# Moving eight merge-gate products ahead of retention, and pooling behind it, in a two-layer hybrid decoder step

## The chip, the cores and the metric

One core of a Trainium2 chip runs the whole step. The metric is the device time of one execution in microseconds (us). TensorE (PE) multiplies, VectorE (DVE) and ScalarE (ACT) work on elements, GpSimd (POOL) does the same more slowly and issues some DMAs, and SyncE (SP) issues the DMAs that load weights.

## The reference, cut to what matters

For each of two layers, over 320 tokens (256 of a prompt, 64 of samples):

```
h = x @ w_in                          # 13824 columns, split into
qa, ka, va, ga, ub, gb, qc, kc, vc, gc, ma, mb, mc = split(h)
ya = (rmsnorm(retention(qa, ka, va)) * silu(ga)) @ w_ret_o
yb = (pool(ub) @ w_pool_map * scale * silu(gb)) @ w_pool_o
yc = (window_attention(qc, kc, vc) * silu(gc)) @ w_att_o
merged = sigmoid(ma) * ya + sigmoid(mb) * yb + sigmoid(mc) * yc
x = layer_norm(alpha * x + merged @ w_out)
```

The three branches do not depend on each other, so their input products may be computed in any order, as long as each branch's parts come in its own order.

## The kernel before, in words

All tensors lie transposed: 128 features on the partitions, 320 tokens along the free axis. Every matrix is cut into 128x128 blocks, and eight blocks form a *chunk* of weights, loaded by one 512 KB DMA that SP issues (`load`, L139). The fp32 product is made of three matmuls on high and low parts. For each chunk ACT makes the high part (`split_h`, L148, tile `h`), a copy rounded to fp32r, and DVE subtracts it from the weight to give the low part (`split_l`, L156, tile `l`). A block then costs three 128x128x320 matmuls (`block`, `block_low`), a chunk 24 of them.

The loop in `run` (from L330) works off a fixed list of output products, `layer_groups()` (L51). In the middle of it each chunk's parts are made two chunks ahead: `split_h(c + 2)` at the start of a chunk, `split_l(c + 2)` and `load(c + 6)` at its middle. A product such as `("ub", 3)` takes 16 blocks (two chunks); `y*` products take 8, `pm` products 2. When a product's last matmul is issued, its `done_` function takes it out of PSUM. What must happen before a product's first block stands in `before` (L462).

Attention and the four retention heads run beside the products in *lanes*: generators whose steps are issued by `pump` (L275) at the end of each chunk. `pump` keeps a planned backlog of ACT, DVE and POOL in `self.busy`, takes `CHUNK_US` off it for each chunk, and steps a lane only if the planned backlogs of ACT and DVE are under `LATE_US`. The pooling of one `ub` product sits in a list called misc, which is stepped at every chunk whatever the backlog. All queues work in the order of the program, so an instruction that waits holds up everything behind it on its engine.

In `split_l` (L156 to L167) the plan may send a low part to POOL: if DVE's planned backlog is over 0.5 and POOL has none.

The order before in each layer: attention's `qc`, `kc`, `vc`; eight `ub` (pooling inputs) directly after them, while the second half of attention is in its lane; then `qa`, `ka`, `va` of four heads, with the eight `pm` (pooling map) products between them; then `gb`; then `mb` and `yb` alternating in pairs; then the same for branches a and c; then `wo`.

`done_mb` (L961) puts the gate's sigmoid into a small tile `sig`; `done_yb` (L969) multiplies it with yb into `acc` (four large tiles, taken at `yb` 0, L471). `done_ub` (L669) copies the product with its history into `ext` and, for the first one, loads `hist` by DMA; `pooling` (L687) forms window sums (`win`, one addition for each doubling of the window: 1, 2, 3 or 4 by group), the result `pp` and its parts `pt`. `done_pm` (L716) scales into `preB`; `gate` (L658) makes silu(g) times the branch and its high and low parts (`gbh`, `gbl`).

Large tiles come from one pool of 24 buffers (`gran`, L100), among them `x` (8 while a layer's inputs are used), attention's and retention's tiles, `hist`, `pout`, `pt`, `preB`, `oA`, `oC`, `acc`. A new tile waits until the previous holder of its buffer is done with.

Of the kernel before, what the change touches and what calls it, by code (L numbers as in the profile page):

```python
# [11 lines left out]
F32 = mybir.dt.float32  # L12
F32R = mybir.dt.float32r
AF = mybir.ActivationFunctionType
ALU = mybir.AluOpType
# [6 lines left out]
T = NP + NB * NT  # L22
# [29 lines left out]
def layer_groups():  # L52

    g = [[("kc", 0), ("vc", 0), ("qc", 0), ("qc", 1)]]
    g += [[("qc", t)] for t in (2, 3)]
    g += [[("kc", 1)], [("vc", 1)]] + [[("qc", t)] for t in (4, 5, 6, 7)]
    late = [("ub", i) for i in range(8)]
    for h in range(HA):
        late += [("qa", h), ("ka", h), ("va", 2 * h), ("va", 2 * h + 1)]
    for i, job in enumerate(late):  # L60
        g.append([job])
        if i in (4, 6, 8, 10):
            g += [[("pm", i - 4)], [("pm", i - 3)]]
    for b in "bac":
        g += [[("g" + b, i)] for i in range(8)]
        for j in range(0, 16, 2):
            g += [[("m" + b, j)], [("m" + b, j + 1)], [("y" + b, j)], [("y" + b, j + 1)]]
    g += [[("wo", j)] for j in range(16)]
    return g


def layer_blocks():

    out = []
    for grp in layer_groups():
        for k in range(n_k(grp[0][0])):
            out += [(kind, i, k) for kind, i in grp]
    return out
# [19 lines left out]
class Step:  # L98
# [57 lines left out]
    def split_l(self, c, parts=((0, CH),)):  # L156
        if c < NCHUNK:
            if c not in self.L:
                lo = self.lp.tile([128, CH, 128], F32R, tag="l", name="l")
                self.L[c] = lo  # L160
            eng = None
            if c > 8 and self.busy["v"] > 0.5 and self.busy["p"] < 0:
                eng = self.nc.gpsimd
            for i, j in parts:
                self.tt(self.L[c][:, i:j], self.raw[c][:, i:j], self.H[c][:, i:j].bitcast(F32), ALU.subtract, eng)
                if j == CH:
                    self.raw.pop(c)  # L167

# [165 lines left out]
    def run(self):  # L334
# [30 lines left out]
        for layer in range(DEPTH):  # L365
            if layer:
                self.begin_layer(layer)
            for grp in layer_groups():
                jobs = [Job(kind, i) for kind, i in grp]
                self.before(jobs[0].kind, jobs[0].i)  # L370
                for k in range(n_k(grp[0][0])):
                    if len(jobs) > 1:
                        self.need_x(min(k + 3, 15))
                    for n, job in enumerate(jobs):
                        if pos == 0:
                            self.split_h(c + 2)
                        if pos == CH // 2:
                            self.split_l(c + 2)
                            self.load(c + 6)
                        self.block(job, k, c, pos)  # L380
                        pos += 1
                        if n == len(jobs) - 1:
                            self.block_low(jobs, k)
                        if pos == CH:
                            pos = 0
                            self.H.pop(c)
                            self.L.pop(c)
                            c += 1
                            self.pump()
# [42 lines left out]

    def begin_layer(self, l):
        self.l, zs = l, getattr(self, "z", None)
        self.gated, self.pt, self.acc, self.sig = {}, {}, None, {}
        self.xk = 0
        self.x_gen = self.x_from_input() if l == 0 else self.norm(l - 1, zs, False)
        self.oC = [None, None]
        self.att = {}
        self.ret = {}  # L440
        self.preB = None
        self.oA = None
# [19 lines left out]
    def before(self, kind, i):  # L462
        if kind[0] == "g" and i == 0:
            for lane in {"gb": (), "ga": ("ret0", "ret1"), "gc": ("att",)}[kind]:
                self.drain(lane)
            self.gated[kind[1]] = self.pair(2, kind)
        if kind == "mb" and i == 0:
            for o, src in (("o_wkc", "ckr"), ("o_wvc", "cvr")):
                self.nc.gpsimd.dma_start(out=self.io[o][self.l], in_=self.io[src][self.l, :, NT:, :])
        if kind == "yb" and i == 0:  # L470
            self.acc = [self.g([128, 4, T], name=f"acc{n}") for n in range(4)]  # L471
        if kind == "yc" and i == 0:
            self.merged = self.pair(4, "mg")
        if kind == "wo" and i == 0:
            self.z = [self.g([128, 4, T], name=f"z{n}") for n in range(4)]
# [488 lines left out]
        self.act(out=t, in_=ps, func=AF.Sigmoid)  # L964
        self.sig[j] = t

    done_mb = done_mc = done_ma

    def done_yb(self, j, ps):  # L969
        self.tt(self.acc[j // 4][:, j % 4, :], self.sig.pop(j), ps, ALU.mult)  # L970

    def done_ya(self, j, ps):
        t = self.m([128, T], name="ya")
# [311 lines left out]
```

## Time and profile before

| | |
|---|---|
| median of 3 runs | 2310.35 us (2309.80 to 2310.91) |
| the profiled execution's own time | 2310.74 us |
| its span, first to last instruction | 2309.0 us |
| busy: PE, DVE, ACT, POOL | 2273.1, 1222.3, 945.8, 182.9 us |
| mean granted TensorE clock | 0.992 |
| weight low parts: made by DVE, by POOL | 562, 35 |

The span is the stretch between the first and the last instruction; 1.7 us of the profiled execution lie around it. Layer 0 ends at about 1144 us, layer 1 repeats the same order. The chain of waits follows the end of the kernel back to what released each step.

### The profile page before, as it was taken

The page shows a single profiled execution, that of the slowest core. Times are in us where ns is not written, and L with a number is a line of the kernel's source. Part 1 is how long each engine was busy: PE and PEld are TensorE (multiplying, and loading weights), DVE is VectorE, ACT ScalarE, POOL GpSimd, SP SyncE. Part 2 cuts the span into 40 slices and gives each one's busy share as a digit, 9 for nine tenths or more (in the row PEclk, how much of TensorE's full clock was granted, in tenths as well). Part 3 has the DMA queues.
Part 4 walks back from the last instruction along what each step waited for, and adds up shares of the span by engine and source line. Part 5 has one row for each costly group of instructions (what it writes and reads, how often), then busy time and mean ns, then how long its engine had stood idle before and what let it go on. Part 6 is the DMA issues. An engine that isn't in the chain of part 4 may idle for free.

```text
span 2309.0 us, 37695 instructions
## 1 busy us (share of the span) xinstructions
PE 2273.1 (98%) x15660; PEld 2218.0 (96%) x15660; DVE 1222.3 (53%) x1826; ACT 945.8 (41%) x1536; POOL 182.9 (8%) x190
## 2 busy tenths in 40 slices
PE   8999999999999999999999999999999999999997
PEld 8997999999999999999998989999999999999997
DVE  4568465443444444446665775553434434444566
ACT  4544445333433343333365444443334333433333
POOL 1114000000000000000031230000000000000001
PEclk9999999999999999999999999999999999999998
DMA  7433455444444444444353344554444444444442
GB/s 274 137 137 131 163 189 179 155 151 146 147 154 150 152 146 153 149 151 151 129 196 119 131 136 153 194 183 150 152 148 154 146 149 143 157 154 146 146 150 98
DMA packets 97628, 354.91 MB, mean 154 GB/s; under 512 B 11521, under 2 KB 11969, under 8 KB 97393
## 3 DMA queue, kind: packets, MB, share of 16 engines
q1 hardware_dynamic: 93312, 335.87, 43.5%
q0 software_dynamic: 4144, 16.64, 2.0%
q8 instruction: 122, 2.00, 0.4%
q14 instruction: 50, 0.40, 0.1%
HBM read 338.51 MB, written 17.88 MB: 154 GB/s over the span
## 4 chain that ended last, share of the span: by engine, by line
PE 93%; DVE 5%; ACT 0%; DMA 0%; issue 0%; SPq 0%; DVEq 0%
PE d L196 87%; PE p L196 4%; DVE win L182 1%; PE p L205 1%; PE p L200 1%; DMA w<-w 0%; DVE sc L191 0%; DVE l L182 0%; DVE s L186 0%; DVE z L182 0%; DVE s L182 0%; DVE s L752 0%; DVE pp L186 0%; DVE sc L186 0%; DVE pp L182 0%
## 5 line engine op out<-in xcount | busy, mean ns | idle before, releaser
L196 PE MATMUL d<-xh,h 128*128 128x320 f32 x3424 | 1073.4, 314 | 15.6 <-ACT xh L175 6.9
L182 DVE TENSOR_TENSOR l<-w,h 128x1024 fp32r<-128x1024 f32 (+1 forms) x562 | 699.3, 1245 | 724.6 <-ACT h L175 723.7
L196 PE MATMUL d<-xh,l 128*128 128x320 f32 x3424 | 1060.5, 310 | 0.9 <-DVE l L182 0.9
L196 PE MATMUL d<-xl,h 128*128 128x320 f32 x3424 | 1050.2, 310 | 0.0
L175 ACT ACTIVATE h<-w 128x1024 fp32r<-128x1024 f32 (+1 forms) x597 | 627.5, 1052 | 495.1 <-PE d L196 363.1
L196 PEld LDWEIGHTS d<-xh,h 128*128 128x128 f32 x3424 | 645.3, 188 | 28.5 <-ACT xh L175 7.8
L196 PEld LDWEIGHTS d<-xh,l 128*128 128x128 f32 x3424 | 645.5, 189 | 2.1 <-DVE l L182 1.8
L196 PEld LDWEIGHTS d<-xl,h 128*128 128x128 f32 x3424 | 642.1, 188 | 0.0
L196 PE MATMUL d<-mgh,h 128*128 128x320 f32 x512 | 158.8, 310 | 0.0
L196 PE MATMUL d<-mgh,l 128*128 128x320 f32 x512 | 158.3, 309 | 0.0
L196 PE MATMUL d<-mgl,h 128*128 128x320 f32 x512 | 158.3, 309 | 0.0
L175 ACT ACTIVATE sig<-d 128x320 f32<-128x320 f32 x96 | 42.0, 437 | 226.0 <-PE d L196 226.0
L182 POOL TENSOR_TENSOR l<-w,h 128x1024 fp32r<-128x1024 f32 x35 | 84.9, 2432 | 226.6 <-ACT h L175 191.5
L196 PEld LDWEIGHTS d<-mgh,h 128*128 128x128 f32 x512 | 96.1, 188 | 0.2
L196 PEld LDWEIGHTS d<-mgh,l 128*128 128x128 f32 x512 | 96.1, 188 | 0.2
L196 PEld LDWEIGHTS d<-mgl,h 128*128 128x128 f32 x512 | 96.1, 188 | 0.0
L182 POOL TENSOR_TENSOR acc<-acc,ya 128x320 f32<-128x320 f32 x32 | 28.2, 880 | 822.2 <-DVE ya L182 822.2
L196 PE MATMUL d<-gch,l 128*128 128x320 f32 x256 | 79.2, 309 | 0.0
L196 PE MATMUL d<-gah,h 128*128 128x320 f32 x256 | 79.2, 309 | 0.0
L196 PE MATMUL d<-gal,h 128*128 128x320 f32 x256 | 79.2, 309 | 0.0
L196 PE MATMUL d<-gbh,h 128*128 128x320 f32 x256 | 79.2, 309 | 0.0
L196 PE MATMUL d<-gcl,h 128*128 128x320 f32 x256 | 79.2, 309 | 0.0
(234 smaller groups left out, 2119.3 us busy)
## 6 DMA issues: line engine op xcount, KB each, us to landing
w<-w SPq DMA_DIRECT2D x595, 512.0 KB, 3.3
s<-s SPq DMA_DIRECT2D x16, 512.0 KB, 5.6
o_rets<-s POOLq DMA_DIRECT2D x16, 512.0 KB, 5.1
bias<-bias_p SPq DMA_DIRECT2D x8, 512.0 KB, 5.5
o_x<-z SPq DMA_DIRECT2D x8, 320.0 KB, 2.2
ck<-ck SPq DMA_DIRECT2D x4, 512.0 KB, 4.7
cv<-cv SPq DMA_DIRECT2D x4, 512.0 KB, 6.1
xin<-x SPq DMA_DIRECT2D x3, 640.0 KB, 11.8
```

Of the source, the lines that this page charges most:

```text
L175: self.nc.scalar.activation(out=out, in_=in_, func=func, **kw)
L182: (eng or self.nc.vector).tensor_tensor(out=out, in0=a, in1=b, op=op)
L196: self.nc.tensor.matmul(out, lhsT=lhsT, rhs=rhs, start=start, stop=stop)
L200: self.nc.tensor.matmul(out, lhsT=lhsT, rhs=rhs, start=False, stop=True, skip_group_check=True)
L205: self.nc.tensor.transpose(out, in_, ident[:n, :n])
```

## The change

In each layer the first eight merge-gate products of branch b (`mb` 0 to 7) come straight after attention's inputs, where the pooling inputs were. Retention's inputs follow, then the pooling inputs in pairs, with `mb` 8 to 11 and the pooling maps between them, then the remaining `mb`; then all `gb`, then all sixteen `yb`. Branches a and c stay as they were.

The gates now go straight into `acc`, which is taken a quarter at a time at `mb` 0, 4, 8 and 12. Gates 0 to 7 are copied raw, and their sigmoid is taken in place, over two tiles of 128x1280, just before `mb` 8; gates 8 to 15 get their sigmoid on the way out of PSUM. `done_yb` multiplies in place. Two DMAs that copy cache rows from HBM to HBM move from `mb` 0 to `gb` 0. Low parts of weights are always made by DVE.

```diff
-    late = [("ub", i) for i in range(8)]
+    late = [("mb", j) for j in range(8)]
     for h in range(HA):
         late += [("qa", h), ("ka", h), ("va", 2 * h), ("va", 2 * h + 1)]
-    for i, job in enumerate(late):
-        g.append([job])
-        if i in (4, 6, 8, 10):
-            g += [[("pm", i - 4)], [("pm", i - 3)]]
-    for b in "bac":
+    for n in range(4):
+        late += [("ub", 2 * n), ("ub", 2 * n + 1), ("mb", 8 + n)]
+        if n:
+            late += [("pm", 2 * n - 2), ("pm", 2 * n - 1)]
+    late += [("mb", 12), ("mb", 13), ("pm", 6), ("pm", 7), ("mb", 14), ("mb", 15)]
+    g += [[job] for job in late]
+    g += [[("gb", i)] for i in range(8)]
+    g += [[("yb", j)] for j in range(16)]
+    for b in "ac":
...
-            eng = None
-            if c > 8 and self.busy["v"] > 0.5 and self.busy["p"] < 0:
-                eng = self.nc.gpsimd
...
-        if kind == "mb" and i == 0:
+        if kind == "gb" and i == 0:
             for o, src in (("o_wkc", "ckr"), ("o_wvc", "cvr")):
...
-        if kind == "yb" and i == 0:
-            self.acc = [self.g([128, 4, T], name=f"acc{n}") for n in range(4)]
+        if kind == "mb" and i % 4 == 0:
+            self.acc.append(self.g([128, 4, T], name=f"acc{i // 4}"))
+        if kind == "mb" and i == 8:
+            for n in range(2):
+                self.act(self.acc[n], self.acc[n], AF.Sigmoid)
...
+    def done_mb(self, j, ps):
+        self.act(self.acc[j // 4][:, j % 4, :], ps, AF.Copy if j < 8 else AF.Sigmoid)
+
     def done_yb(self, j, ps):
-        self.tt(self.acc[j // 4][:, j % 4, :], self.sig.pop(j), ps, ALU.mult)
+        a = self.acc[j // 4][:, j % 4, :]
+        self.tt(a, a, ps, ALU.mult)
```

## Rows read from the trace of the kernel before

**Rows 1.** The page's first part: busy time, share of the span, instructions.

```profile
PE 2273.1 (98%) x15660; PEld 2218.0 (96%) x15660; DVE 1222.3 (53%) x1826; ACT 945.8 (41%) x1536; POOL 182.9 (8%) x190
```

**Rows 2.** Waits of PE: total us, times, longest.

```profile
PE d L196 <- ACT xh L175: 6.9, 3, 5.0
PE d L196 <- DVE rt L182: 6.7, 2, 3.3
```

**Rows 3.** Windows: length, PE, PEld, DVE, ACT, POOL busy, clock, DMA share, GB/s.

```profile
60.00:140.00 80.00, 80.00 (x565) 72.45 (x564) 44.34 (x109) 40.52 (x107) 8.98 (x9) 1.00 0.41 137
160.00:180.00 20.00, 19.33 (x117) 17.09 (x116) 19.34 (x36) 9.54 (x34) 8.17 (x4) 1.00 0.30 106
180.00:200.00 20.00, 18.66 (x133) 16.14 (x131) 19.41 (x39) 8.28 (x20) 9.73 (x5) 1.00 0.29 99
200.00:220.00 20.00, 16.23 (x122) 15.18 (x123) 19.17 (x49) 10.00 (x30) 9.52 (x8) 1.00 0.35 120
240.00:400.00 160.00, 160.00 (x1193) 151.06 (x1192) 90.03 (x161) 76.48 (x138) 10.69 (x20) 1.00 0.53 180
1300.00:1320.00 20.00, 19.52 (x119) 17.35 (x119) 19.30 (x40) 9.92 (x33) 7.19 (x3) 1.00 0.29 95
1320.00:1340.00 20.00, 19.05 (x137) 16.76 (x135) 19.41 (x40) 8.95 (x23) 9.35 (x4) 1.00 0.27 91
1340.00:1360.00 20.00, 16.53 (x108) 15.11 (x109) 19.20 (x46) 10.11 (x30) 11.03 (x9) 0.83 0.40 133
```

**Rows 4.** The timeline of PE around its longest stop in layer 1.

```profile
1341.96 0.31 PE L196 MATMUL d<-pt,h 128*128 128x320 f32 x1
1345.61 0.64 PE L196 MATMUL d<-xh,h 128*128 128x320 f32 x1 [3.34 <-DVE rt L182]
```

**Rows 5.** Windows of PE alone, then of all engines at the norm: PEclk of stretches.

```profile
1344.60:1351.40 6.80, 5.79 (x37) 0.51 0.37 145
...
1150.00:1160.00 10.00, 8.73 (x42) 8.59 (x42) 9.19 (x16) 7.57 (x14) 10.00 (x11) 0.65 0.01 2
```

**Rows 6.** Timelines of DVE and POOL: start, us, instruction, xcount.

```profile
194.79 0.63 DVE L182 TENSOR_TENSOR win<-ext 128x454 f32<-128x454 f32 x1
195.45 6.04 DVE L182 TENSOR_TENSOR win<-win 128x452 f32<-128x452 f32 x3
...
195.08 5.27 POOL L182 TENSOR_TENSOR l<-w,h 128x1024 fp32r<-128x1024 f32 x2 [8.28 <-ACT h L175]
...
1331.56 1.94 DVE L182 TENSOR_TENSOR win<-win 128x452 f32<-128x452 f32 x3
```

**Rows 7.** Groups by line and form, with the tile view's POOL row second.

```profile
L182 DVE TENSOR_TENSOR l<-w,h 128x1024 fp32r<-128x1024 f32 x560 | 697.9, 1247 | 717.2 <-ACT h L175 716.2 <-issue 0.3
...
L182 POOL TENSOR_TENSOR l<-w,h x35: 2342/2401/2760, 90.9 to 1364.5; 128x1024 fp32r<-128x1024 f32 x35
...
L175 ACT ACTIVATE h<-w 128x1024 fp32r<-128x1024 f32 x595 | 626.3, 1054 | 490.5 <-PE d L196 363.1 <-issue 93.1 <-ACT h L175 16.8
L175 ACT ACTIVATE sig<-d 128x320 f32<-128x320 f32 x96 | 42.0, 437 | 226.0 <-PE d L196 226.0
L175 ACT ACT_TABLE_LOAD x26 | 33.4, 1283 | 11.0 <-PE d L196 9.9 <-PEq L1259 0.7
```

**Rows 8.** The chain of waits: start, us, what (products of later stages).

```profile
404.68 637.12 PE d L196 x4344
```

**Rows 9.** Groups of pooling's instructions on DVE; the second is the tile view's.

```profile
L182 DVE TENSOR_TENSOR win<-ext 128x454 f32<-128x454 f32 x16 | 10.0, 623 | 0.0
...
L182 DVE TENSOR_TENSOR win<-win x24: 617/629/2708, 142.5 to 1343.6; 128x452 f32<-128x452 f32 x12, 128x448 f32<-128x448 f32 x8, 128x440 f32<-128x440 f32 x4
...
L191 DVE TENSOR_SCALAR preB<-d,pscale 128x320 f32<-128x320 f32 x16 | 8.0, 542 | 0.0
...
L182 DVE TENSOR_TENSOR pt<-pp,pt 128x320 fp32r<-128x320 f32 x16 | 7.7, 482 | 0.0
L186 DVE SCALAR_TENSOR_TENSOR pp<-win,ext 128x256 f32<-128x256 f32 x16 | 6.8, 426 | 0.7
```

**Rows 10.** DVE's timeline where the first pooling history is loaded, layer 0.

```profile
123.24 0.22 DVE L679 COPY ext<-hist 128x120 f32<-128x120 f32 x1 [5.89 <-DMA hist<-pool]
```

**Rows 11.** Timelines of ACT and DVE at layer 0's last gb product.

```profile
411.76 0.44 ACT L175 ACTIVATE gt<-d 128x320 f32<-128x320 f32 x1 [2.41 <-PE d L196]
...
413.25 0.49 DVE L182 TENSOR_TENSOR gbl<-gt,gbh 128x320 fp32r<-128x320 f32 x1 [0.54 <-ACT gbh L175]
```

**Rows 12.** Timelines of POOL and DVE at the start of layer 1.

```profile
1174.16 5.02 POOL L182 TENSOR_TENSOR l<-w,h 128x1024 fp32r<-128x1024 f32 x2 [0.63 <-ACT h L175]
...
1171.30 8.23 DVE L182 TENSOR_TENSOR xl<-z,xh 128x320 fp32r<-128x320 f32 x4
```

**Rows 13.** Issues of retention's output DMA: xcount, KB, us to landing.

```profile
o_rets<-s POOLq DMA_DIRECT2D x16, 512.0 KB, 5.1
```

More of the change, by code (lines that the diff above doesn't have):

```diff
@@ L160, in split_l @@
                 self.L[c] = lo
-            eng = None
-            if c > 8 and self.busy["v"] > 0.5 and self.busy["p"] < 0:
-                eng = self.nc.gpsimd
             for i, j in parts:
-                self.tt(self.L[c][:, i:j], self.raw[c][:, i:j], self.H[c][:, i:j].bitcast(F32), ALU.subtract, eng)
+                self.tt(self.L[c][:, i:j], self.raw[c][:, i:j], self.H[c][:, i:j].bitcast(F32), ALU.subtract)
                 if j == CH:
@@ L434, in begin_layer @@
         self.l, zs = l, getattr(self, "z", None)
-        self.gated, self.pt, self.acc, self.sig = {}, {}, None, {}
+        self.gated, self.pt, self.acc, self.sig = {}, {}, [], {}
         self.xk = 0
@@ L965, in done_ma @@
         self.sig[j] = t
-    done_mb = done_mc = done_ma
+    done_mc = done_ma
+    def done_mb(self, j, ps):
+        self.act(self.acc[j // 4][:, j % 4, :], ps, AF.Copy if j < 8 else AF.Sigmoid)
     def done_yb(self, j, ps):
-        self.tt(self.acc[j // 4][:, j % 4, :], self.sig.pop(j), ps, ALU.mult)
+        a = self.acc[j // 4][:, j % 4, :]
+        self.tt(a, a, ps, ALU.mult)
     def done_ya(self, j, ps):
```

## Prediction

> **What bounds the kernel now.** The first part of the page comes first: PE is busy for 2273 of the 2309 us of the span, no other engine for much over half of it [rows 1]. So the order of the products matters only where PE stands still or works slowly, and the most that a new order can give is what PE loses. The waits of PE say where. Two lines carry most: 6.9 us for `xh`, which belong to the first products of the two layers and aren't touched, and 6.7 us in two stops of 3.3 us for `rt`, the rotary step of retention [rows 2]. They are found by the table of windows. In 60 to 140 us (first half of attention) and 240 to 400 us (retention) PE is busy the whole time, with DVE at 55% and 56%. In 160 to 220 us of layer 0 and 1300 to 1360 us of layer 1 DVE is busy for 19.2 to 19.4 of every 20 us, and PE falls to 16.2 [rows 3]. There the second half of attention and the pooling of eight `ub` products run beside each other. DVE is the bound for 60 us of each layer, and PE waits for it.
>
> Why DVE is full is seen in its timeline. Three window additions take 1.94 us where nothing disturbs them and 6.04 us where POOL makes two low parts at the same time; two of the three took their own time plus all that POOL needed [rows 6]. So a low part that POOL makes, 2.40 us [rows 7], holds up DVE for about 2.05 us ((6.04 - 1.94) / 2), while DVE itself would have made it in 1.25 us. In this stretch POOL's help costs DVE more than it saves.
>
> **What PE loses there.** Layer 0: 0.67 + 1.34 + 3.77 = 5.78 us of idle time in the three windows. Layer 1: 0.48 + 0.95 + 3.47 = 4.90 us [rows 3]. In layer 1 the 3.34 us stop [rows 4] is followed by a stretch at the lower clock: 0.51 of full speed, which is 1.2 GHz, for 6.8 us, in which PE was busy for 5.79 us [rows 5]. At full clock that work takes half, so 2.9 us more are lost. Sum: 13.6 us. It is a little low, because matmuls overlap: a wide one lasts 0.31 us in the timeline [rows 4] but follows the last one after 637.12 / 4344 = 0.147 us [rows 8], so each stop hides 0.16 us more. With some 7 stops in each layer (an estimate) that is 0 to 2.2 us; I take the middle, 1.1.
>
> **The change part by part.** The matmuls are the same, so the sum is made of stops alone. A chunk costs 24 x 0.147 = 3.52 us.
>
> *Attention's second half beside `mb` 0 to 7.* Eight products are 16 chunks, 56 us without the lane's own matmuls. DVE gets 16 low parts (20 us), while the pooling goes; ACT's copy of a gate is priced by the sigmoid of the same size, 0.44 us each [rows 7]. The nearest row is the first half of attention: 55% DVE, no PE idle time. I expect the same, so all of the 13.6 us go. The low end is that none does.
>
> *POOL's 35 low parts return to DVE.* 35 x 1.25 = 43.6 us of DVE work come back, and up to 35 x 2.05 = 72 us of being held up go. Cost on PE: 0; the cover is DVE's free 45% in the stages where they now fall. At the start of layer 1, three of them lie within the normalisation: four `xl` took 8.23 us beside POOL [rows 12]. On DVE alone they take four of about 0.48 us (the `pt` row of the same shape, [rows 9]) and three of 1.25, 5.7 us. Zero, with 0 to 1 us as bounds. The Trainium skill speaks against this part: Perfetto Trace Analysis, section Optimizing Scalar/DVE Operations, says that offloading even to GpSimd may make sense if DVE is saturated, though the two share a read port. By its first half DVE would have 43.6 us more and PE would lose; this trace follows its second half.
>
> *Pooling after retention.* Per `ub`, DVE needs 0.62 for the first window addition, 0.63 for each further one (0 to 3, 0.94 on average), 0.43 for `pp`, 0.48 for `pt`, 0.54 for `preB` [rows 9], and some 0.75 in small pieces (an estimate from the same listing): 3.8 us, 30 us for eight. The stretch of 8 `ub`, 4 `mb` and 6 `pm` has 25.5 chunks, 90 us. The retention row stands for its other work, 56% [rows 3]; 30 / 90 adds 33%, 89% while the last head is still in its lane, under that after it. So DVE is not full, but close: 0 to 3 us per layer, and I take 0.3. The first history load makes DVE wait 5.89 us [rows 10]; that happens today in a window without PE idle time, and the weight parts are two chunks (7 us) ahead, so 0.
>
> *ACT at `mb` 8.* Two sigmoids of 1280 columns stand ahead of the next high part. From 437 ns for 320 columns and 1054 for 1024, one takes about 1.3 us; with a table load of 1.28 [rows 7] ACT is occupied for 3.9 us. The high part ends at 3.9 + 1.05 and the low part at 6.2 us of the 7.0 that two chunks give. Behind them stand the next product's copy and the lane's. 0 to 2 us per layer; I take 0.3, since nothing else must be late at the same time.
>
> *`yb` directly after `gb`.* The last `gb` is needed by the eighth block of `yb` 0, 7 x 3 x 0.147 = 3.1 us after its own last matmul. From that matmul to the end of `gbl` it is about 2.2 us (413.74 less some 411.6, [rows 11]). 0; bounds 0 to 1 us per layer. The sixteen `yb` follow each other with one multiplication each per 3.52 us. The two HBM copies of POOL's queue at `gb` 0 stand ahead of nothing that anyone waits for there: 0, and so is the removal of their issue at `mb` 0.
>
> *Large buffers.* The `acc` tiles now hold 2 of the 24 buffers during retention (as `preB` did) and 3 to 4 during pooling. The queue that could suffer is SP's, since `hist` must wait for a buffer and the weight loads stand behind it. A buffer's last holder is at worst a state that is being written out, 5.1 us [rows 13], and loads run at least three chunks ahead. 0; bounds 0 to 3 us per layer.
>
> Sum: 13.6 + 1.1 - 2 x (0.3 + 0.3) = 13.5 us. The profiled execution took 2310.74 us, which gives 2297.2; the median of the runs is 0.4 lower, so **2297 us**.
>
> **The rivals.**
>
> *The stop moves to pooling (12%).* If the 89% are really 95% and more, as today, PE waits there again. Half of the gain would be left: 2310.4 - 6.8 = 2303.6. For it speaks that four window additions per `ub` come in a burst at the end; against it, that the last head has left by then and that no low part of POOL stretches them.
>
> *Table loads (5%).* Retention's square roots now lie between the sigmoids of `mb` 8 to 15. If each of two square roots brought two extra loads, that is 4 x 1.28 = 5.1 us of ACT per layer, and if all of it showed on PE, 2297 + 10.3 = 2307.3, hardly a change. Against it: today's square roots already lie between the silus of `gb`, and 26 loads are made [rows 7]; counted by the new order I get fewer, some 20 to 22. The Trainium skill's ScalarE: Activation LUTs, section Table sets: the hidden batching unit, tells to batch calls by table set, which the new order breaks here and mends at `gb`; its 2.7 us per switch would make that 10.8 us per layer, but the row says 1.28.
>
> *Slower (7%).* A full pool holds up SP at `hist`, and the weight loads with it. It decides from the point at which the wait exceeds the loads' lead, about 3 chunks or 10.6 us. [...] A wait of 20 us would cost 9.4 + 2.9 = 12.3 per layer, 24.6 in all: 2297 + 24.6 = 2321.6. Against it speaks that a buffer needs only work that is already queued, and a state's 5.1 us.
>
> *The change does little (4%):* PE's stops belong to retention's first rotary step itself and come back wherever it stands: 2310. The windows 240 to 400, with three more such steps and no idle time, speak against it.
>
> **How the numbers follow.** The forecast has 72%. Its own range reaches from 2294.5 (13.6 + 2.2, no new cost) to 2301. The norm's half-clock stretch [rows 5] isn't touched, but where it begins may shift; 2 us for that bring the low end to 2292.5. The high end, 2305, takes in the first rival. About 0.2%, 4.6 us, is what a measurement here can tell from no change: faster by more is the forecast and the first rival, 84%; within it are the table loads and the do-little case, 9%; slower 7%.
>
> **What would show it.** Right: in the windows from 120 to 220 and from 1270 to 1360 us PE has no idle time and DVE stands at 50 to 70%; no `l` on POOL; `win` never over 0.7 us; no half clock near 1345 us; 20 to 22 table loads. Wrong: DVE at 95% or PE idle time in the new pooling stretch (some 90 us long, after the last `va`), a stop right after the two large sigmoids, a wait of SP at `hist`, a stop at the eighth block of `yb` 0, or a PE wait on `xl` at the start of layer 1.

## The result, and the profile after

The changed kernel takes **2294.7 us** (median of 4 runs, 2294.02 to 2294.78) against 2310.12 us for the kernel before (4 runs, 2309.80 to 2310.91). The ratio is 0.9931, with a 95% interval from 0.9916 to 0.9946: 15.4 us faster. The forecast was 2297 us, with a range from 2292.5 to 2305. The profiled execution took 2294.67 us, its span is 2292.8 us.

The page's first part, after, answers to [rows 1]:

```profile
PE 2265.2 (99%) x15660; PEld 2213.3 (97%) x15660; DVE 1207.3 (53%) x1861; ACT 944.2 (41%) x1534; POOL 99.4 (4%) x155
```

One number here says more than it seems to. DVE took back 35 low parts, which are 35 x 1.247 = 43.6 us of work, and yet its busy time *fell* from 1222.3 to 1207.3 us. So 43.6 + 15.0 = 58.6 us of what [rows 1] call busy had been DVE held up by POOL: 1.67 us for each of the 35 parts. The run in which only these parts move, below, gives nearly the same (DVE 1205.9 us busy, so 60.0 us of hold).

The waits of PE, after (total us, times, longest), answer to [rows 2]. The two stops for `rt` are gone, and no line of their size has come in their place:

```profile
PE d L197 <- ACT xh L176: 7.6, 3, 4.5
PE p L197 <- DVE S L183: 2.2, 2, 1.1
PE d L197 <- DVE l L183: 1.4, 2, 0.9
```

The windows, after, in the columns of [rows 3]: first those of the stretches in which PE lost time before, then those in which pooling now stands.

```profile
160.00:180.00 20.00, 20.00 (x125) 18.08 (x124) 12.51 (x31) 9.71 (x30) 0.00 (x0) 1.00 0.30 106
180.00:200.00 20.00, 20.00 (x160) 17.55 (x159) 13.84 (x38) 10.88 (x28) 1.96 (x4) 1.00 0.32 106
200.00:220.00 20.00, 20.00 (x136) 18.40 (x135) 11.39 (x33) 11.86 (x32) 0.64 (x1) 1.00 0.56 184
...
1340.00:1360.00 20.00, 20.00 (x143) 17.76 (x142) 10.65 (x27) 10.72 (x31) 0.00 (x0) 1.00 0.54 184
...
360.00:400.00 40.00, 39.95 (x284) 38.98 (x285) 29.35 (x62) 19.33 (x36) 1.61 (x3) 1.00 0.53 175
400.00:440.00 40.00, 40.00 (x275) 40.00 (x274) 27.10 (x47) 16.72 (x32) 1.67 (x3) 1.00 0.56 182
```

PE is busy throughout, DVE fell from 19.3 of 20 us to between 11 and 14, and at 1340 us the granted clock is 1.00 (0.83 before). The new pooling stretch keeps DVE at 73% and 68%, and PE loses 0.05 us of its 80.

Where the time went is read from the last output product's last matmuls, one row for each layer. PE's timeline, before:

```profile
1144.11 0.31 PE L196 MATMUL d<-mgl,h 128*128 128x320 f32 x1
...
2287.84 0.31 PE L196 MATMUL d<-mgl,h 128*128 128x320 f32 x1
```

The same two of PE's timeline, after:

```profile
1137.68 0.31 PE L197 MATMUL d<-mgl,h 128*128 128x320 f32 x1
...
2272.46 0.31 PE L197 MATMUL d<-mgl,h 128*128 128x320 f32 x1
```

Layer 0 is shorter by 6.43 us, layer 1 by 8.95 (1143.73 before, 1134.78 after), and the tail behind the last matmul by 0.8. Of layer 1's figure about 1 us is not the change's: the granted clock was half for 10.2 us in the norm between the layers before and for 6.8 us here. That length differs between executions of one and the same kernel: a later trace of the changed kernel (of the series with the median of 2294.06 us, below) has 10.2 us there too, and its layer 1 took 1135.73 us, 0.95 more than here.

### The profile page after: what moved, and what is told of

It reads as the page before. It is cut to its first block, busy times and chain, and to the rows that moved or that the text cites. A ratio compares the mean times of both kernels' runs of the same rounds, so it can differ in the third digit from the quotient of the medians.

```text
span 2292.8 us, 37711 instructions
## 1 busy us (share of the span) xinstructions
PE 2265.2 (99%) x15660; PEld 2213.3 (97%) x15660; DVE 1207.3 (53%) x1861; ACT 944.2 (41%) x1534; POOL 99.4 (4%) x155
## 4 chain that ended last, share of the span: by engine, by line
PE 97%; DVE 1%; ACT 1%; DMA 1%; SPq 0%; issue 0%
PE d L197 91%; PE p L197 5%; PE p L206 1%; PE p L201 1%; DMA w<-w 1%; DVE z L183 0%; ACT acc L176 0%; DVE l L183 0%; ACT h L176 0%; ACT L176 0%; SPq L340 0%; DVE z L194 0%; ACT z L176 0%; SPq L150 0%; DVE pp L187 0%
## 5 line engine op out<-in xcount | busy, mean ns | idle before, releaser
L183 DVE TENSOR_TENSOR l<-w,h 128x1024 fp32r<-128x1024 f32 (+1 forms) x597 | 737.8, 1237 | 719.9 <-ACT h L176 719.2
L176 ACT ACTIVATE sig<-d 128x320 f32<-128x320 f32 x64 | 28.0, 438 | 149.7 <-PE d L197 149.7
L197 PE MATMUL d<-gbh,l 128*128 128x320 f32 x256 | 79.1, 309 | 0.0
L197 PE MATMUL d<-gbl,h 128*128 128x320 f32 x256 | 79.1, 309 | 0.0
L197 PE MATMUL d<-gah,l 128*128 128x320 f32 x256 | 79.1, 309 | 0.0
L197 PE MATMUL d<-gch,h 128*128 128x320 f32 x256 | 79.1, 309 | 0.0
```

Of the source, the lines that this page charges most:

```text
L176: self.nc.scalar.activation(out=out, in_=in_, func=func, **kw)
L183: (eng or self.nc.vector).tensor_tensor(out=out, in0=a, in1=b, op=op)
L197: self.nc.tensor.matmul(out, lhsT=lhsT, rhs=rhs, start=start, stop=stop)
```

## The experiments

The change has two parts that can be had separately: a new order of products, and low parts made by DVE alone. The forecast gave all of the gain to the first. So the first question was what each part does alone.

### Old order, all low parts on DVE

The plan's books are left as they were, so that every instruction stands in the order of before; only the engine of the 35 parts is another.

```diff
+            if eng is not None:
+                self.busy["p"] += 0.15 + CH * 128 / 380.0
+                self.busy["v"] -= 0.15 + CH * 128 / 960.0
...
-                self.tt(self.L[c][:, i:j], self.raw[c][:, i:j], self.H[c][:, i:j].bitcast(F32), ALU.subtract, eng)
+                self.tt(self.L[c][:, i:j], self.raw[c][:, i:j], self.H[c][:, i:j].bitcast(F32), ALU.subtract)
```

> The order of before, instruction for instruction (the plan still books the 35 parts on POOL), but DVE makes them. My theory, that in the crowded stretch POOL's parts cost DVE more than they save: 10.6 parts per layer (25.5 us of POOL at 2.40) take 10.6 x (2.05 - 1.25) = 8.5 us off DVE, so it falls from 58 to about 49 of 60 us, and most of PE's 13.6 us of stops go: 2298 to 2303 us, no half clock near 1345 us. Rival, that POOL did carry work that DVE has no room for: the stops grow by some 10.6 x 1.25 = 13 us per layer, 2315 to 2335 us. Rival, that only the order counts: within 2 us of before.

Measured: **2294.64 us** (2294.04 to 2296.46, 5 runs), ratio 0.9934, 0.9922 to 0.9947. This is the changed kernel's time, without one product moved. Its windows over the two stretches:

```profile
160.00:220.00 60.00, 59.56 (x411) 53.60 (x411) 54.69 (x146) 34.40 (x102) 2.84 (x6) 1.00 0.43 135
1300.00:1360.00 60.00, 59.74 (x426) 53.76 (x425) 51.78 (x136) 34.22 (x100) 2.85 (x6) 1.00 0.48 150
```

The kernel before, same windows:

```profile
160.00:220.00 60.00, 54.23 (x370) 48.41 (x369) 57.93 (x122) 27.81 (x84) 27.42 (x15) 1.00 0.31 108
1300.00:1360.00 60.00, 55.10 (x361) 49.22 (x361) 57.92 (x124) 28.99 (x85) 27.57 (x15) 0.94 0.32 107
```

And the same stretch of the low parts `l` alone, first before, and below it this kernel (PE, PEld and DVE, before also POOL):

```profile
160.00:220.00 60.00, 29.41 (x95) 17.72 (x95) 2.13 (x1) 25.47 (x11) 1.00 0.31 108
```

```profile
160.00:220.00 60.00, 32.35 (x105) 19.65 (x105) 15.78 (x13) 1.00 0.43 135
```

Before, DVE spent 57.93 - 2.13 = 55.80 us on everything but low parts; here 54.69 - 15.78 = 38.91, though it got further. The 16.9 us between them, for 25.47 / 2.40 = 10.6 parts on POOL, are 1.6 us of hold per part. A part on DVE costs it 1.23. DVE is still 91% busy over the stretch, the order is the old one, and PE stands still for 0.44 us in place of 5.77. The additions that stood ahead of `rt` show it in one row: `win<-win` x3 took 6.04 us before [rows 6]. DVE's timeline here:

```profile
191.68 1.94 DVE L185 TENSOR_TENSOR win<-win 128x452 f32<-128x452 f32 x3
...
195.98 0.48 DVE L185 TENSOR_TENSOR rt<-d,rot 128x320 f32<-128x320 f32 x1
```

Before, `rt` came at 202.37 us. Until then DVE had not taken the product out of PSUM, and PE waited; that is one of the two stops of 3.3 us in [rows 2].

The Trainium skill's Perfetto Trace Analysis, section Optimizing Scalar/DVE Operations, allows offloading from a saturated DVE even to GpSimd, with the reservation that the two share a read port, so that it might not help. For this kernel, whose DVE was 97% busy in the two stretches, this pair of runs decides for the reservation: the offload cost 15 us.

### New order, with POOL's parts again

```diff
+            eng = None
+            if c > 8 and self.busy["v"] > 0.5 and self.busy["p"] < 0:
+                eng = self.nc.gpsimd
...
-                self.tt(self.L[c][:, i:j], self.raw[c][:, i:j], self.H[c][:, i:j].bitcast(F32), ALU.subtract)
+                self.tt(self.L[c][:, i:j], self.raw[c][:, i:j], self.H[c][:, i:j].bitcast(F32), ALU.subtract, eng)
```

> The new order with the old rule for POOL's parts put back. My theory, that with pooling apart from attention DVE has room for either: 2294.5 to 2298 us, a few parts on POOL, windows additions held up to 2.7 us where they meet one, no stop of PE over 1 us. Rival, that the parts on POOL were the whole cause and the order none: half of the gain or more goes, 2302 us and up.

Measured: **2294.49 us** (2293.17 to 2295.73, 5 runs), ratio 0.9932, 0.9918 to 0.9945. The new order with the old rule gives the whole gain too. The two do not add. The plan still sends 19 parts to POOL, and they still hold DVE up. The tile view's row of `win`, min/median/max in ns:

```profile
L186 DVE TENSOR_TENSOR win<-win x24: 618/628/2724, 372.6 to 1566.6; 128x452 f32<-128x452 f32 x12, 128x448 f32<-128x448 f32 x8, 128x440 f32<-128x440 f32 x4
```

Its windows in attention's second half have room for that, 13.4 of 20 us:

```profile
160.00:180.00 20.00, 20.00 (x123) 17.88 (x122) 13.50 (x35) 10.56 (x36) 2.40 (x1) 1.00 0.29 87
180.00:200.00 20.00, 20.00 (x166) 18.00 (x165) 13.30 (x37) 11.19 (x31) 5.55 (x4) 1.00 0.29 98
```

The order also changes what the rule sends. In the windows of the low parts alone, POOL makes 4 in this stretch (9.67 us), where it made 11 before (25.47):

```profile
160.00:220.00 60.00, 29.69 (x97) 18.07 (x96) 9.14 (x8) 9.67 (x4) 1.00 0.37 116
```

So the loss needed both: a stretch that fills DVE, and POOL's work that holds it up there. Either part of the change takes one of them away. How much of the order's share comes from the room on DVE and how much from the fewer parts on POOL, this run doesn't separate.

### Pooling beside attention after all, diluted

The `ub` go back beside attention, alternating with `mb` 0 to 7, maps between them; `mb` 8 to 15 follow retention. POOL makes no parts.

```diff
-    late = [("mb", j) for j in range(8)]
+    late = []
+    for n in range(8):
+        late += [("ub", n), ("mb", n)]
+        if n % 2 and n > 1:
+            late += [("pm", n - 3), ("pm", n - 2)]
...
+    late += [("mb", j) for j in range(8, 16)]
```

> Pooling inputs back beside attention's second half, but each followed by a gate product, so that the stretch has 32 chunks instead of 16; DVE makes all parts. My theory, that what counts is DVE's work per time of PE: attention 20 us, pooling 30, 32 parts 40 make 90 of some 120 us, 75%, and PE has hardly a stop: 2294.5 to 2298 us. Rival, that attention and pooling get in each other's way whatever the room (queues, bursts): stops of 3 us and more per layer come back, 2301 us and up.

Measured: 2293.53 us (2292.44 to 2294.36, 4 runs), ratio 0.9928, 0.9915 to 0.9942. Its windows:

```profile
160.00:180.00 20.00, 20.00 (x126) 18.09 (x125) 14.69 (x39) 10.43 (x34) 0.00 (x0) 1.00 0.32 106
...
200.00:220.00 20.00, 20.00 (x154) 19.54 (x153) 15.65 (x45) 11.58 (x30) 0.00 (x0) 1.00 0.40 130
```

Pooling beside attention is not itself a loss: diluted, and with no parts on POOL, it stops PE nowhere in these windows. What moving it behind retention is worth can't be read from this run, since DVE making all parts gives the whole gain by itself.

### Sigmoid directly out of PSUM

The in-place sigmoids ahead of `mb` 8 were costed at 0.3 us per layer, table loads at 0 (with a rival at +10.3 us).

```diff
-        if kind == "mb" and i == 8:
-            for n in range(2):
-                self.act(self.acc[n], self.acc[n], AF.Sigmoid)
...
-        self.act(self.acc[j // 4][:, j % 4, :], ps, AF.Copy if j < 8 else AF.Sigmoid)
+        self.act(self.acc[j // 4][:, j % 4, :], ps, AF.Sigmoid)
```

> The changed kernel, with the sigmoid of gates 0 to 7 taken at once on the way out of PSUM instead of in place before gate 8, so that it falls between attention's exponentials. Up to 16 more table loads per layer at 1.28 us, 20 us of ACT in some 60 us, on top of 10 to 12 of 20 us. My theory, that ACT has this room and the parts are two chunks ahead: 2294.5 to 2299 us, 45 to 52 loads. Rival, that table loads fall on PE: up to 2 x 20 us, 2310 to 2335 us.

> The direct sigmoid again, with more rounds, beside the changed kernel on the same chip: 1 to 2.5 us faster than it if the large sigmoids before gate 8 cost what the traces show (0.5 us per layer and the start and norm by chance), no difference otherwise.

Measured: 2292.72 us (2292.28 to 2294.46, 4 runs), and in the repeat 2293.4 (2292.70 to 2293.43, 5 runs; ratio 0.9926, 0.9914 to 0.9939), beside the changed kernel again on the same chip:

> The changed kernel, for the comparison with the direct sigmoid: 2294 to 2295 us.

It measured 2294.77 us (2294.02 to 2295.79, 5 runs; ratio 0.9933, 0.9920 to 0.9945). The runs of the repeat and of the changed kernel beside it don't overlap, their ratio intervals do: some 1.4 us faster, by runs alone, and the lowest median here. Groups of table loads, first after, then direct sigmoid:

```profile
L176 ACT ACT_TABLE_LOAD x20 | 25.7, 1283 | 10.9 <-PE d L197 9.9 <-PEq L1268 0.7
```

```profile
L176 ACT ACT_TABLE_LOAD x36 | 46.2, 1283 | 16.1 <-PE d L197 14.8 <-PEq L1265 0.7
```

36 loads, fewer than the 45 to 52 expected. The 16 extra ones are 20.5 us of ACT, and a window of the repeat shows some of them (15.09 us of ACT for 9.71 after) with PE still full:

```profile
160.00:180.00 20.00, 20.00 (x125) 18.08 (x125) 11.83 (x28) 15.09 (x34) 0.00 (x0) 1.00 0.29 95
```

So the rule of batching calls by table set (the Trainium skill, ScalarE: Activation LUTs, Table sets: the hidden batching unit) saved nothing here, where ACT is 41% busy. The run takes away the two large sigmoids and adds the loads at once, so it shows their balance and not the price of either.

### POOL's subtractions alone: what holding DVE up costs

In place of POOL's part, DVE makes it, and POOL repeats the subtraction into the spent weight tile at the same 35 places. Nobody waits for that result as data. If the late parts were the harm, this is nearly free; if the holding up of DVE is, it must be worse than before, because DVE has the parts too.

```diff
...
+            if eng is not None:
+                self.nc.gpsimd.tensor_tensor(
+                    out=self.raw[c][:], in0=self.raw[c][:], in1=self.H[c][:].bitcast(F32), op=ALU.subtract
+                )
...
```

> The old order, DVE makes all parts (2294.6 us), and at the 35 places of before POOL does a subtraction of the same size whose result nobody reads (it goes over the weight tile that is done with; the next load into that tile waits for it). Theory A, that what stopped PE was DVE held up by POOL's reads: DVE had 54.7 of 60 us to do; 10.6 x 2.05 = 22 us more make 76 of 60, PE stops for 10 to 20 us per layer, 2315 to 2335 us, slower than before, since DVE still makes the parts. Theory B, that the stops came from the parts themselves being late (2.4 us on POOL instead of 1.25): nothing waits for the dummy, 2294 to 2298 us.

Measured: **2340.45 us** (2340.27 to 2341.69, 4 runs), ratio 1.0133, 1.0118 to 1.0148. More than expected, and 45.8 us over the same kernel without POOL's subtractions. Waits of PE:

```profile
PE d L204 <- DVE rt L190: 11.2, 2, 5.8
PE d L204 <- DVE l L190: 10.4, 6, 3.1
PE p L213 <- DVE sc L199: 8.1, 8, 1.9
```

A window of it:

```profile
200.00:220.00 20.00, 13.55 (x92) 10.55 (x91) 19.06 (x34) 7.46 (x22) 7.47 (x5) 0.74 0.30 107
```

The same stop, `rt`, is there with 11.2 us for 6.7, and the granted clock at 0.74 with it. No data of POOL's was awaited, so it is POOL's work beside DVE that does it. The size was underestimated because the clock was left out. By the traces PE is idle for 56.1 us here and for 28.2 without the subtractions; these 27.9 us lie within the 20 to 40 expected for both layers. PE's busy time grew by 17.8 us more for the same matmuls (2282.5 for 2264.7), with a mean granted clock of 0.986 for 0.994. The repeat also keeps a weight tile in use for longer. ACT, which uses a loaded tile first, shows no cost of that: it waited 10.1 us for weight DMAs here and 12.1 us without the subtractions.

### The same load in either order: two attempts that missed

If the new order gives DVE room, it should bear a regular load of POOL's work better than the old one. First POOL's repeat of the subtraction came at every second of the first 112 chunks of each layer, in the old and in the new order, beside the changed kernel again. Against the experiment above, only the condition differs (in the new order, the same lines are added to the changed kernel):

```diff
-            if eng is not None:
+            if c > 8 and c % 2 == 0 and c % (NCHUNK // DEPTH) < 112:
```

> The old order with DVE's parts, and the same dummy on POOL at every second chunk of the first 112 of each layer (some 54 per layer, 8 of them in the crowded stretch of 16 chunks). Theory A: 8 x 2.05 = 16 us more on DVE's 54.7 of 60: 5 to 12 us of stops per layer, 2305 to 2320 us. Theory B: 2294 to 2298 us.

> The new order with the same dummies at the same chunks. DVE is at 50 to 70% in all of its windows, and one dummy per two chunks adds at most 2.05 of 8 us, 26%: if the order's worth is room on DVE, PE hardly stops: 2294.5 to 2299 us, and the new order beats the old one by 6 us or more under the same load. If the order gives no room, both are equally slow.

> The changed kernel again, on the chip of the three others: 2294 to 2295 us.

Measured: old order 2340.96 us (2339.98 to 2341.97; ratio 1.0134, 1.0117 to 1.0151), new order **2389.4** (2387.86 to 2390.71; ratio 1.0343, 1.0328 to 1.0359), the changed kernel 2294.06 (ratio 0.9932, 0.9917 to 0.9947). The expectation for the new order, 2294.5 to 2299, is missed by 90 us. The waits of all engines in 485 to 560 us, new order, show stops that the question was not about:

```profile
ACT h L181 <- PE d L202: 50.4, 11, 5.0
...
PE d L202 <- ACT h L181: 11.7, 10, 1.2
PEld d L202 <- DVE l L188: 10.7, 10, 1.1
PE d L202 <- DVE l L188: 8.5, 10, 0.8
```

Here, behind the 112th chunk, POOL's added work is over. ACT waits for a tile `h` until PE has used it, and PE then waits for ACT and DVE: a pattern with too little lead that keeps itself going for ten stops. POOL's repeats hold weight and `h` tiles longer and may have brought it on; that was not tested by itself.

So the load was made of two subtractions of 128x512 into a spare tile that nobody waits for (room for it came from the pool of mini tiles, 4 in place of 6):

```diff
+            if c > 8 and c % 2 == 0 and c % (NCHUNK // DEPTH) < 112:
+                for _ in range(2):
+                    self.nc.gpsimd.tensor_tensor(out=self.spare, in0=self.dmask, in1=self.qdec, op=ALU.subtract)
```

> The old order with DVE's parts. At every second chunk of the first 112 of each layer POOL does two subtractions of two constant tiles (128x512 each, together the size of a part) into a tile of their own, so that no weight or part tile is held by them. Theory A, DVE is held up by POOL's reads: 8 such pairs at up to 2.05 us in the crowded stretch, 16 us on DVE's 54.7 of 60; 5 to 12 us of stops per layer, 2303 to 2320 us, and windows additions up to 1.9 us. Theory B, that the last dummies cost time through the weight tiles that they held: 2294 to 2297 us.

> The new order with the same dummies. If its worth is room on DVE: 2294.5 to 2300 us, no stop over 1 us in attention's or pooling's stretch. If the order gives no room: within 3 us of the old order with the same dummies.

Measured: old order 2337.01 us (2336.38 to 2337.44; ratio 1.0115, 1.0100 to 1.0131), new order 2339.6 (2337.99 to 2340.58; ratio 1.0126, 1.0112 to 1.0140). The expectation for the new order missed again. Windows, first of the old order, then of the new one:

```profile
160.00:260.00 100.00, 94.04 (x649) 84.54 (x648) 78.82 (x171) 46.27 (x127) 18.71 (x19) 0.97 0.38 124
```

```profile
160.00:260.00 100.00, 100.00 (x715) 90.53 (x714) 65.43 (x132) 47.85 (x119) 20.91 (x19) 1.00 0.39 131
...
360.00:400.00 40.00, 30.63 (x218) 28.76 (x216) 37.85 (x45) 17.08 (x32) 30.23 (x22) 0.94 0.38 124
```

In attention's second half the expectation holds: with much the same load (POOL busy for 18.71 and 20.91 us) PE loses 6 us in the old order and none in the new. The old order's 6.3 us before `sp_r` in each layer lie in retention. And the new order has its full stretch elsewhere. POOL's and then PE's timeline, new order:

```profile
365.49 0.56 POOL L623 DMA_DIRECT2D o_retp<-a  x1 [19.91 <-DVE a L190]
...
373.03 29.55 POOL L171 TENSOR_TENSOR spare<-dmask,qdec 128x512 f32<-128x512 f32 x18
```

```profile
403.20 0.64 PE L200 MATMUL d<-xh,h 128*128 128x320 f32 x1 [12.30 <-DVE preB L195]
```

POOL's queue stood behind retention's output DMA for 19.91 us, and then 18 subtractions ran without a gap, beside pooling. DVE, 73% busy in 360 to 400 us of the changed kernel, went to 95%, and PE stopped for 12.30 us before an input product, until DVE had taken a map product out of PSUM (`preB`). The new order did not remove the risk; it has pooling, the two-input work, beside something else. In the changed kernel the stop doesn't arise, since POOL makes no parts at all.

Left open: an order without the eight gates ahead (retention beside attention) was not tried.

## Why the prediction was right, point by point

- **What bounds.** Right: PE's lost time was the whole prize, and it was found where DVE was full. In the windows of [rows 3] PE is idle after for 0.23 us, before `sp_r`, a tile of retention; its other waits are those of the kernel's start and the norms. The signs came too: DVE is busy for 63% of 160 to 220 us, and the longest `win` takes 0.63 us.
- **The stops, 13.6 + 1.1 us.** Right. By layers the sum says 5.78 + 0.55 = 6.3 and 4.90 + 2.9 + 0.55 = 8.35. Measured are 6.43 and, without the norm's 0.95 us, 8.0: 14.4 for 14.7.
- **Which part brings it.** Added in the forecast's order, its prices held: the new order with POOL's rule left in has the whole gain (2294.49), and taking POOL's parts away adds nothing to it (2294.7). What it had wrong is the account of the cause. It put all 13.6 us on attention's second half beside `mb` 0 to 7 and "Zero, with 0 to 1 us as bounds" on POOL's 35 parts, and this second part alone is worth the same 15 us (2294.64). Its own reading of [rows 6], that POOL's help costs DVE more than it saves, pointed there and was not carried into the sum. The total came out all the same, because it was added up from what PE loses, and that can be won back only once.
- **Hold per part.** 2.05 us, from one row, was a little high: 1.67 over the whole kernel, 1.6 in the stretch.
- **Pooling after retention.** DVE was forecast at 89%, and is at 73 and 68%. Pooling's own work was sized rightly: of DVE's 63.82 us in 345 to 435 us, some 28 are pooling (30 reckoned) and 29.79 are 25 low parts. The term that was too large is retention's: 56% carried over the work of retention's heads (some 44 us in 240 to 400 us, beside 42.81 of low parts), and only some 6 us of the last head are left here. The 0.3 us per layer is not seen: PE is idle for 0.23 us.
- **ACT at `mb` 8.** 2.43 us for both sigmoids, as reckoned (2 x 1.3), and the low part behind them ends at 357.22 us, 5.9 after the table load began, for 6.2 reckoned. PE's only stop between 330 and 450 us is that of 0.23 us for `sp_r`. So these 0.3 us per layer aren't seen as a stop either, though direct sigmoids are a little faster. ACT's timeline, after:

```profile
351.29 1.28 ACT L176 ACT_TABLE_LOAD   x1
352.58 2.43 ACT L176 ACTIVATE acc<-acc 128x1280 f32<-128x1280 f32 x2
354.92 1.04 ACT L176 ACTIVATE h<-w 128x1024 fp32r<-128x1024 f32 x1
```

DVE's low part behind it, after:

```profile
355.99 1.23 DVE L183 TENSOR_TENSOR l<-w,h 128x1024 fp32r<-128x1024 f32 x1 [5.35 <-ACT h L176]
```

- **`yb`, buffers, history, start of layer 1.** Zero, as said: PE's waits have no line for `gbl`, DVE waits 9.5 us for `hist` in both layers together (11.3 before) without a stop of PE, and two `xl` take 0.88 us where four took 8.23 [rows 12].
- **Table loads.** 20, of the 20 to 22 forecast. The rival falls with the 36 loads that cost nothing on balance.
- **The rival "slower".** No such wait came. Its 2.9 us for the clock were read from layer 1 alone and are not shown as the price of every such stop: layer 0 has a stop of 3.3 us as well ([rows 2]), and its granted clock stays at 1.00 in 200 to 220 us [rows 3].
- **The sum.** 16.2 us of span against 13.5. The 2.7 us between them are 1.2 of new costs that did not come, 0.95 of the norm's half clock and 0.8 of the tail, less 0.3 by which the stops gave less than reckoned. The norm's share stood in the low end of the range, "2 us", and is chance. The tail's was not foreseen, and no run explains it.

## What to carry to other kernels

Where a profile shows DVE at 95% and more beside a busy POOL, part of DVE's busy time may be waiting: look for instructions of one shape whose longest is several times the median (2708 against 629 ns, [rows 9]), and take POOL's work away before moving anything else. Where a loss needs two causes, removing either one gives the whole gain, so price each part of a change alone as well as against what is left after the other, and don't add the two gains. POOL's work behind a waiting DMA in its queue came out all at once here, where the wait ended.

## What the runs showed of the hardware

**A one-input operation can be held too.** The Trainium skill (SBUF — State Buffer, Who interferes with whom) says that DVE's two-SBUF-input operations contend with GpSimd's reads, and copies and `tensor_scalar` where they run in a 2-port mode. The first agrees: `win<-win` takes 0.63 us alone and up to 2.7. The second is seen here in fp32. POOL's and then DVE's timeline with POOL's repeated subtractions in the old order:

```profile
196.73 2.41 POOL L170 TENSOR_TENSOR w<-w,h 128x1024 f32<-128x1024 f32 x1 [4.57 <-DVE l L190]
```

```profile
197.10 2.45 DVE L199 TENSOR_SCALAR sc<-sc,s 128x256 f32<-128x256 f32 x2
```

Two such `sc` take 0.62 us in the kernel before. Their rate suggests such a mode: after the change, `sc` takes 282 ns for 128 columns and 351 for 256, so 0.54 ns for a column more, while the two-input `kx` and `qx`, 419 ns for 256 columns and 685 for 512, take 1.04, nearly twice as long. An operation with one input in PSUM was not held: in the new order DVE's two `s<-s,p` ran beside POOL's subtractions (369.17 to 372.10 us) in the 1.28 us that two take in the changed kernel:

```profile
370.87 1.27 DVE L190 SCALAR_TENSOR_TENSOR s<-s,p 128x512 f32<-128x512 f32 x2
```

That it is POOL's reads and not its writes was tested by no run, but a row bears on it. A MEMSET of POOL reads no tile, and a two-input operation beside it took its usual 0.49 us, in both layers. POOL's and then DVE's timeline, old order with all parts on DVE, layer 0:

```profile
196.81 0.54 POOL L513 MEMSET vp<- 128x512 f32 x1
```

```profile
196.90 0.49 DVE L185 TENSOR_TENSOR a<-rt,sw 128x320 f32<-128x320 f32 x1
```

**Beside a POOL without gaps, small DVE instructions can take as long as large ones.** DVE's timeline in the new order beside the 18 subtractions:

```profile
385.31 1.28 DVE L687 COPY ext<-hist 128x120 f32<-128x120 f32 x1
...
393.74 1.37 DVE L190 SCALAR_TENSOR_TENSOR pp<-win,ext 128x256 f32<-128x256 f32 x1
395.03 1.22 DVE L186 TENSOR_TENSOR s<-win,cnt 128x3 f32<-128x3 f32 x1
396.28 0.16 DVE L186 TENSOR_TENSOR pp<-s,ext 128x3 f32<-128x3 f32 x1
```

The first three take 0.22 [rows 10], 0.43 [rows 9] and some 0.16 us alone. Whatever their size, they last 1.2 to 1.4 us here, close to the 29.55 / 18 = 1.64 us of one subtraction; the fourth got through in its usual time. So under such a load the *number* of DVE's small instructions counts for more than their size.

**Stops can keep themselves going.** In the run of 2389.4 us PE waited 10 times in 485 to 560 us for ACT's high part, after POOL's added work had ended. ACT had waited for PE 11 times, 4.6 us each on average. PE lost 21 of those 75 us (busy 53.70, POOL 0.00), and the pattern ended only near 560 us. That the chain had lost its lead is read from these waits, and was not tested by a run.
